# Softmax times values on one core: table load ahead of the wait, and the value copies of the next pass moved into the last head

## The chip, the cores and the metric

The kernel runs on one core of one Trainium2 chip. The metric is device time in microseconds (us), the median of several executions. "DVE" is VectorE, "ACT" ScalarE, "PE" TensorE, "POOL" GpSimd, and "SP" the engine that issues the DMAs. In the views "PEld" is the loading of weights into PE, and a "q" behind a name (SPq) stands for that engine's instruction queue.

## The reference

For 8 x 12 = 96 heads it takes a 1024 x 1024 score matrix and a 1024 x 64 value matrix, in float32:

```python
scores_max = np.max(scores, axis=-1, keepdims=True)
attn = np.exp(scores - scores_max)
attn = attn / (np.sum(attn, axis=-1, keepdims=True) + 1e-8)
return np.matmul(attn, v).astype(np.float32)
```

The kernel leaves the maximum out (the scores are normal random numbers) and gets the row sums from an extra column of ones beside the values.

## The kernel before

A loop of 24 passes handles four heads (k = 0 to 3) per pass, each head in eight rows of tiles (r = 0 to 7). Each row goes through ACT (exp), PE (eight transposes into PSUM, where its results land), DVE (copy to `pt`), PE (eight matmuls with the values) and, once or twice per head, DVE (reciprocal and product, `normalise`). Matmuls of a row are issued two rows late (`LAG = 2`). Each of the four heads has one 4 MB score buffer, which SP refills for the next pass once its exp is done.

The values are loaded for four heads at once (`load_v`), cast to float16 by POOL (`cast_v`), and "spread" by DVE: four copies per head put them into that head's `vones` buffer.

```python
    def spread_v(k, s, behind=None):
        copy = nc.vector.tensor_copy(
            out=vones_bufs[k][s * Q : (s + 1) * Q, :, 0:D].rearrange(
                "i (h l) d -> i h l d", l=L
            ),
            in_=v_half[k * Q : (k + 1) * Q, :, s],
        )
        if behind is not None:
            after(copy, behind)
...
    def heads(n0):
        for k in range(AHEAD):
            if k == 0:
                for s in range(S):
                    spread_v(k, s)              # four copies at the head of the pass
            st = dict(vones=vones_bufs[k])
            for r in range(R):
                ...                             # exp of two rows, eight transposes
                pt = take(pt_bufs)
                copy = nc.vector.tensor_copy(out=pt[:], in_=psT[:])
                if k < AHEAD - 1 and r % (R // S) == 0:
                    spread_v(k + 1, r // (R // S), copy)    # the next head's, in every second row
                ...
                pending.append((n0, k, r, pt, st))
                if len(pending) > LAG:
                    finish(pending.pop(0))      # matmuls, and normalise at the end of a head
        while pending:
            finish(pending.pop(0))
        cast_v()
        last(n0)                                # loads for the next pass, second store
```

`last` has a special case for the last pass but one: it cuts the final head's load into pieces of four, two, one and one rows, so that the end of the run need not wait for a whole tile.

The softmax here doesn't subtract the row's maximum and nothing guards it: scores larger than these inputs give would overflow.

Of the kernel before, what the change touches and what calls it, by code (L numbers as in the profile page):

```python
# [9 lines left out]
FP16 = mybir.dt.float16  # L10
EXP = mybir.ActivationFunctionType.Exp
# [3 lines left out]
def kernel(  # L15
# [6 lines left out]
    nc = tc.nc  # L22
    P = 128
# [6 lines left out]
    R = SQ // P  # L30
# [5 lines left out]
    AHEAD = 4  # L36
    Q = P // AHEAD
    S = P // Q
# [16 lines left out]
    sb_pool = ctx.enter_context(tc.tile_pool(name="sbpool", bufs=1))  # L55
# [4 lines left out]
    order16 = const_pool.tile([P, P], FP16, name="order16")  # L60

    nc.vector.tensor_copy(  # L62
        out=order16[:].rearrange("p (t j) -> p t j", t=T),
        in_=ident32[:].rearrange("p (j t) -> p t j", t=T),
# [11 lines left out]
    def buffers(pool, count, shape, dtype, name):  # L76
        return [pool.tile(shape, dtype, name=f"{name}{k}") for k in range(count)]

    s_bufs = buffers(sb_pool, AHEAD, [P, R, SK], FP32, "s_nat")
    v_sb = sb_pool.tile([P, C // L, S, L, D], FP32, name="v_sb")  # L80
    v_half = sb_pool.tile([P, C // L, S, L, D], FP16, name="v_half")
    p_bufs = buffers(sb_pool, 8, [P, EB, SK], FP16, "p_nat")
    pt_bufs = buffers(sb_pool, 4, [P, SK], FP16, "pt")
    out_bufs = buffers(sb_pool, 2, [P, T, R, D], FP32, "out_sb")
# [8 lines left out]
    def take(bufs):  # L93
        k = turn.get(id(bufs), 0)
        turn[id(bufs)] = k + 1
        return bufs[k % len(bufs)]
# [4 lines left out]
    def after(a, b):  # L101

        tc.add_manual_dep(
            a.ins,
            b.ins.name,
            mybir.DependencyInfo(mybir.DependencyClass.NoSync, mybir.DependencyReason.DATA),
            reason="order",
        )

    def queue(dma):  # L110

        if queued:
            after(dma, queued[-1])
        queued.append(dma)
# [4 lines left out]
    def normalise(k, st, first, last):  # L119

        psO = psO_whole if k % 2 == 0 else psO_banks[first]
        psO = psO[:, :, 0 : G * M].rearrange("p b (g m) -> p b g m", m=M)
        recip = st["recip"][:, first:last]
        nc.vector.reciprocal(out=recip, in_=psO[:, :, :, D : D + 1])  # L124
        h = k % T
        for t in range(T):
            part = slice(t * W, (t + 1) * W)
            rows = st["out_sb"][h * W : (h + 1) * W, t, first * G : last * G, :]
            nc.vector.tensor_tensor(  # L129
                out=rows.rearrange("j (b g) d -> j b g d", g=G),  # L130
                in0=psO[part, :, :, 0:D],
                in1=recip[part].to_broadcast([W, last - first, G, D]),
                op=mybir.AluOpType.mult,
            )

    def finish(u):

        n0, k, r, pt, st = u
        b, g = r // G, r % G
        if r == 0:  # L140
            st["recip"] = take(rc_bufs)
            st["out_sb"] = out_bufs[k // T]
        bank = psO_whole[:, b] if k % 2 == 0 else psO_banks[b][:, 0]
        for c in range(C):
            nc.tensor.matmul(  # L145
                out=bank[:, g * M : (g + 1) * M],
                lhsT=pt[:, c * P : (c + 1) * P],
                rhs=st["vones"][:, c, 0:M],
                start=(c == 0),
                stop=(c == C - 1),  # L150
            )
        if k % 2 == 1:
            if g == G - 1:
                normalise(k, st, b, b + 1)
        elif r == R - 1:
            normalise(k, st, 0, R // G)
        if r == R - 1 and k == T - 1:
            store(n0, 0)

    def store(n0, k):  # L160

        rows = out_bh.rearrange("(m x) y -> m x y", x=P)
        dma = nc.sync.dma_start(
            out=rows[bass.ds((n0 + k) // T, 1)].rearrange("o x y -> (o x) y"),
            in_=out_bufs[k // T][:].rearrange("x t r d -> x (t r d)"),
        )
        for other in stores:
            apart(dma, other)
            apart(other, dma)
        apart(dma, dma)  # L170
        stores.append(dma)
        queue(dma)
# [8 lines left out]
    def load(k, n, parts=(R,), r=0, **cond):  # L181
        for rows in parts:
            queue(
                nc.sync.dma_start(  # L184
                    out=s_bufs[k][:, r : r + rows, :],
                    in_=one(sc_bh, n)[:, r : r + rows, :],
                    **cond,
                )
            )
            r += rows  # L190

    def load_v(n):

        rows = v_bh.rearrange("(m x) y -> m x y", x=P)
        queue(
            nc.sync.dma_start(  # L196
                out=v_sb[:].rearrange("x h s l d -> x (h s l d)"),
                in_=rows[bass.ds(n // AHEAD, 1)].rearrange("o x y -> (o x) y"),
            )
        )  # L200

    def cast_v():
        nc.gpsimd.tensor_copy(out=v_half[:], in_=v_sb[:])  # L203
# [12 lines that stand above are left out]
    def load_next(k, n0):  # L216

        if k < AHEAD - 2:
            load(k, (n0 + (AHEAD + k)) % BH, cond=n0 < BH - AHEAD)

    def last(n0):


        before = queued[-1:]

        with tc.If(n0 < BH - 2 * AHEAD) as cmp:  # L226
            queued[:] = before
            load(AHEAD - 2, (n0 + (2 * AHEAD - 2)) % BH)
            load_v((n0 + 2 * AHEAD) % BH)
            load(AHEAD - 1, (n0 + (2 * AHEAD - 1)) % BH)  # L230
            store(n0, AHEAD - T)
        with cmp.Else():
            with tc.If(n0 < BH - AHEAD) as cmp2:
                queued[:] = before
                load(AHEAD - 2, BH - 2, (4, 4))
                load(AHEAD - 1, BH - 1, (4,))
                store(n0, AHEAD - T)
                load(AHEAD - 1, BH - 1, (2, 1, 1), 4)
            with cmp2.Else():
                queued[:] = before  # L240
                store(n0, AHEAD - T)

    def heads(n0):

        for k in range(AHEAD):
            if k == 0:
                for s in range(S):
                    spread_v(k, s)
            st = dict(vones=vones_bufs[k])
            for r in range(R):  # L250
                if r % EB == 0:
                    p_nat = take(p_bufs)
                    rows = 1 if k == AHEAD - 1 and r == R - EB else EB
                    for g in range(0, EB, rows):
                        nc.scalar.activation(  # L255
                            out=p_nat[:, g : g + rows, :].rearrange(
                                "p r (x v) -> p x r v", v=Q * L
                            ),
                            in_=s_bufs[k][:, r + g : r + g + rows, :].rearrange(
                                "p r (i x l) -> p x (r i) l", i=Q, l=L  # L260
                            ),
                            func=EXP,
                        )
                p_row = p_nat[:, r % EB, :].rearrange("p (h q l) -> p h l q", q=P, l=L)
                psT = take(psT_bufs)
                for c in range(C):
                    nc.tensor.transpose(  # L267
                        out=psT[:, c * P : (c + 1) * P],
                        in_=p_row[:, c // L, c % L, :],
                        identity=order16[:],  # L270
                    )
                pt = take(pt_bufs)
                copy = nc.vector.tensor_copy(out=pt[:], in_=psT[:])  # L273
                if k < AHEAD - 1 and r % (R // S) == 0:
                    spread_v(k + 1, r // (R // S), copy)
                if r == R - 1:
                    load_next(k, n0)
                pending.append((n0, k, r, pt, st))
                if len(pending) > LAG:
                    finish(pending.pop(0))  # L280
        while pending:
            finish(pending.pop(0))
        cast_v()
        last(n0)

    assert BH % AHEAD == 0 and BH >= 2 * AHEAD and SK == Q * S * C
    load_v(0)
    for k in range(AHEAD):
        load(k, k)
    cast_v()  # L290
    load_v(AHEAD)
    with tc.For_i(0, BH, AHEAD, iteration_sync="reg_based") as n0:  # L292
        queued.clear()
        heads(n0)
# [30 lines left out]
```

## Time and profile before

| | before |
|---|---|
| time, median of the first 3 executions | 1065.76 us (1065.69 to 1065.81) |
| span of the profile | 1064.0 us |
| a pass in the middle of the run | 43.69 us |
| DMA share and rate in that pass | 1.00, 432 GB/s |
| busiest compute engine | DVE, 74% |
| bytes of a pass | 18.87 million |

The DMA moves 18.87 MB per pass at 432 GB/s, and that takes the whole pass. The compute engines have 11 us of slack or more in each pass and matter only where the DMA has nothing left to do, at the end of the run.

### The profile page before, as it was taken

The numbers are of one execution on the slowest core, as the hardware profiler recorded it, in microseconds if no ns is written. First come the engines' busy times: TensorE is split into PE (matmuls) and PEld (weight loads), VectorE is DVE, ScalarE is ACT, GpSimd is POOL, SyncE is SP. The second block draws the span as 40 slices with busy tenths as digits, with TensorE's granted clock in tenths as the row PEclk, the third lists the DMA queues.
The fourth block names the chain that finished last, engine by engine and source line by source line (L and its number), as shares of the span: only waits on it lengthen the run. The fifth ranks groups of instructions, "written<-read, shape, count | busy, mean of one in ns | idle before, by whom it ended". The sixth has DMA issues, their size and how long they took to land.

```text
span 1064.0 us, 32161 instructions
## 1 busy us (share of the span) xinstructions
PE 731.4 (69%) x12288; PEld 678.4 (64%) x12288; DVE 786.6 (74%) x1589; ACT 735.6 (69%) x432; POOL 48.1 (5%) x31
## 2 busy tenths in 40 slices
PE   2766766767766677677686776867666777666676
PEld 2665756667666667666575665767565666666675
DVE  3776876868768777677786776868768687687777
ACT  3766776666767668586676866667766668676685
POOL 0000000000000000000000000000000000000000
PEclk9888888878889888888988888888889788898989
DMA  9999999999999999999999999999999999999995
GB/s 397 431 418 434 426 433 434 433 434 432 432 434 432 425 443 430 429 431 428 433 431 436 432 434 434 431 434 424 441 427 434 432 426 435 432 432 428 440 425 236
DMA packets 24772, 453.06 MB, mean 426 GB/s; under 512 B 2752, under 2 KB 2752, under 8 KB 9152
## 3 DMA queue, kind: packets, MB, share of 16 engines
q1 hardware_dynamic: 24768, 453.00, 99.2%
q8 instruction: 4, 0.07, 0.0%
HBM read 436.21 MB, written 25.17 MB: 434 GB/s over the span
## 4 chain that ended last, share of the span: by engine, by line
DMA 81%; ACT 12%; issue 3%; ACTq 1%; PE 1%; DVE 0%; SPq 0%; PEld 0%; DVEq 0%
DMA s_nat<-in_scores_dram 81%; ACT p_nat L255 12%; PE psT L267 1%; ACTq L255 1%; ACTq L226 0%; ACTq L292 0%; PE psO L145 0%; DVE pt L273 0%; PE psO_whole L145 0%; SPq L184 0%; PEld L267 0%; ACTq L320 0%; DVE out_sb L129 0%; SPq L196 0%; PEld L145 0%
## 5 line engine op out<-in xcount | busy, mean ns | idle before, releaser
L255 ACT ACTIVATE p_nat<-s_nat 128x2048 f16<-128x2048 f32 (+1 forms) x408 | 704.8, 1799 | 228.1 <-DMA s_nat<-in_scores_dram 202.2
L267 PE MATMUL psT<-order,p_nat 128*128 128x128 f16 x6144 | 574.9, 246 | 269.9 <-ACT p_nat L255 263.9
L273 DVE COPY pt<-psT 128x1024 f16<-128x1024 f16 x768 | 515.8, 687 | 200.6 <-PE L267 109.4
L267 PEld LDWEIGHTS <-p_nat 128*128 128x128 f16 x6144 | 446.5, 123 | 298.3 <-ACT p_nat L255 295.7
L145 PEld LDWEIGHTS <-pt 128*128 128x128 f16 x6144 | 302.9, 107 | 81.0 <-DVE pt L273 77.7
L145 PE MATMUL psO<-vones,pt 128*128 128x65 f16 x3072 | 177.4, 201 | 53.9 <-DVE pt L273 50.2
L145 PE MATMUL psO_whole<-vones,pt 128*128 128x65 f16 x3072 | 189.9, 211 | 2.7 <-DVE pt L273 2.4
L207 DVE COPY vones<-v_half 32x512 f16<-32x512 f16 x384 | 109.4, 285 | 22.8 <-POOL v_half L203 6.0
L255 ACT ACT_TABLE_LOAD x24 | 30.8, 1283 | 89.8 <-DMA s_nat<-in_scores_dram 81.7
L203 POOL CAST v_half<-v_sb 128x2048 f16<-128x2048 f32 x25 | 47.4, 1896 | 1002.3 <-DVE vones L207 957.1
L129 DVE TENSOR_TENSOR out_sb<-psO,recip 64x256 f32<-64x256 f32 x192 | 81.1, 423 | 6.1
L129 DVE TENSOR_TENSOR out_sb<-psO_whole,recip 64x512 f32<-64x512 f32 x96 | 66.1, 688 | 3.0
L124 DVE RECIPROCAL recip<-psO 128x4 f32<-128x4 f32 x96 | 17.1, 178 | 34.4 <-PE psO L145 17.6
L124 DVE RECIPROCAL recip<-psO_whole 128x8 f32<-128x8 f32 x48 | 9.7, 203 | 4.5 <-PE psT L267 3.9
L71 DVE MEMSET vones<- 128x16 f16 x4 | 0.2, 72 | 0.8 <-PEq L309 0.8
L62 DVE CAST order<-ident 128x128 f16<-128x128 f32 x1 | 0.2, 227 | 0.4 <-POOL ident masks.py:199 0.4
masks.py:199 POOL TENSOR_SCALAR_AFFINE_SELECT ident<-ident 128x128 f32<-128x128 f32 x1 | 0.3, 295 | 0.1
masks.py:197 POOL MEMSET ident<- 128x128 f32 x1 | 0.2, 205 | 0.3 <-POOLq L309 0.3
L309 POOL MEMSET const-float32-0.0<- 128x1 f32 x1 | 0.1, 100 | 0.2 <-issue 0.2
L309 POOL MEMSET const-bfloat16-1.0<- 128x1 bf16 x1 | 0.1, 103 | 0.0
L309 POOL MEMSET const-uint8-127<- 128x1 uint8 x1 | 0.1, 103 | 0.0
L309 POOL MEMSET const-float32-1.0<- 128x1 f32 x1 | 0.1, 100 | 0.0
## 6 DMA issues: line engine op xcount, KB each, us to landing
s_nat<-in_scores_dram SPq DMA_DIRECT2D x96, 4096.0 KB, 35.8
v_sb<-in_v_dram SPq DMA_DIRECT2D x24, 1024.0 KB, 33.1
out_dram<-out_sb SPq DMA_DIRECT2D x48, 512.0 KB, 26.9
s_nat<-in_scores_dram SPq DMA_DIRECT2D x3, 2048.0 KB, 32.4
s_nat<-in_scores_dram SPq DMA_DIRECT2D x1, 1024.0 KB, 25.4
s_nat<-in_scores_dram SPq DMA_DIRECT2D x2, 512.0 KB
```

The costliest lines, as they stand in the source:

```text
L62: nc.vector.tensor_copy(out=order16[:].rearrange("p (t j) -> p t j", t=T), in_=ident32[:].rearrange("p (j t) -> p t j", t=T),)
L71: nc.vector.memset(vo[:, :, D : D + 2], 1.0)
L124: nc.vector.reciprocal(out=recip, in_=psO[:, :, :, D : D + 1])
L129: nc.vector.tensor_tensor(out=rows.rearrange("j (b g) d -> j b g d", g=G), in0=psO[part, :, :, 0:D], in1=recip[part].to_broadcast([W, last ...
L145: nc.tensor.matmul(out=bank[:, g * M : (g + 1) * M], lhsT=pt[:, c * P : (c + 1) * P], rhs=st["vones"][:, c, 0:M], start=(c == 0), stop=(c ...
L203: nc.gpsimd.tensor_copy(out=v_half[:], in_=v_sb[:])
L207: copy = nc.vector.tensor_copy(out=vones_bufs[k][s * Q : (s + 1) * Q, :, 0:D].rearrange("i (h l) d -> i h l d", l=L), in_=v_half[k * Q : ( ...
L255: nc.scalar.activation(out=p_nat[:, g : g + rows, :].rearrange("p r (x v) -> p x r v", v=Q * L), in_=s_bufs[k][:, r + g : r + g + rows, :] ...
L267: nc.tensor.transpose(out=psT[:, c * P : (c + 1) * P], in_=p_row[:, c // L, c % L, :], identity=order16[:],)
L273: copy = nc.vector.tensor_copy(out=pt[:], in_=psT[:])
L309: nc = _bacc.Bacc("TRN2", target_bir_lowering=False, num_devices=1)
```

## The change

It has two aims. First, the exp table is loaded once per pass. The load stands ahead of the first exp, behind that exp's wait for data. A one-column exp that needs no data is put in front and takes the table load into the wait. Second, four spread copies at the head of each pass delay the first row's work on DVE. They are made earlier: the values of heads 0 and 1 of the next pass are spread during head 3 of this one. For that, heads 2 and 3 get theirs in heads 0 and 1, and the cast moves to the end of head 1.

```diff
+    spare = sb_pool.tile([P, 1], FP16, name="spare")
...
     def heads(n0):
+        table = nc.scalar.activation(out=spare[:], in_=order16[:, 0:1], func=EXP)
         for k in range(AHEAD):
-            if k == 0:
-                for s in range(S):
-                    spread_v(k, s)
...
-                        nc.scalar.activation(
+                        exp = nc.scalar.activation(
...
+                        if k == r == g == 0:
+                            after(exp, table)
...
-                if k < AHEAD - 1 and r % (R // S) == 0:
-                    spread_v(k + 1, r // (R // S), copy)
+                if k < 2 and r % 2 == 0:
+                    spread_v(k + 2, r // 2, copy)
+                elif k == AHEAD - 1:
+                    spread_v(r // S, r % S, copy)
...
+            if k == 1:
+                cast_v()
         while pending:
             finish(pending.pop(0))
-        cast_v()
         last(n0)
...
     cast_v()
+    for k in range(2):
+        for part in range(S):
+            spread_v(k, part)
     load_v(AHEAD)
```

More of the change, by code (lines that the diff above doesn't have):

```diff
@@ L280, in heads @@
                     finish(pending.pop(0))
+            if k == 1:
+                cast_v()
         while pending:
             finish(pending.pop(0))
-        cast_v()
         last(n0)
+    assert AHEAD == S == 4 and R == 2 * S
     assert BH % AHEAD == 0 and BH >= 2 * AHEAD and SK == Q * S * C
```

## The prediction

> **What bounds the kernel now.** I read the page first: busy shares, then the row of DMA shares in forty slices. No compute engine is above 74%. The DMA row is at nine tenths in every slice but the last, and one queue takes nearly all of the sixteen engines' time.
>
> ```profile
> PE 731.4 (69%) x12288; PEld 678.4 (64%) x12288; DVE 786.6 (74%) x1589; ACT 735.6 (69%) x432; POOL 48.1 (5%) x31
> ...
> DMA  9999999999999999999999999999999999999995
> ...
> q1 hardware_dynamic: 24768, 453.00, 99.2%
> ```
>
> An average can hide a pause at each pass of the loop, and the change is aimed at exactly such a place. So the second view was the busy time by stretch. Columns: stretch, its length, busy time (and count) of PE, PEld, DVE, ACT, POOL; then PE clock, DMA share, GB/s. The first two rows are whole passes, the others the end of the run.
>
> ```profile
> 500.00:543.69 43.69, 30.75 (x518) 28.53 (x516) 32.71 (x66) 30.60 (x19) 1.90 (x1) 0.85 1.00 432
> ...
> 923.70:967.40 43.70, 30.51 (x512) 28.45 (x512) 32.73 (x66) 30.62 (x19) 1.90 (x1) 0.85 1.00 432
> ...
> 1046.00:1050.00 4.00, 3.01 (x61) 2.70 (x62) 3.88 (x8) 3.94 (x3) 0.92 (x1) 1.00 0.83 344
> 1050.00:1055.00 5.00, 4.42 (x95) 4.07 (x92) 4.84 (x9) 3.55 (x3) 0.98 (x1) 1.00 0.33 137
> 1055.00:1059.00 4.00, 1.37 (x26) 0.92 (x24) 3.12 (x9) 0.00 (x0) 0.00 (x0) 1.00 0.00 0
> ```
>
> A pass takes 43.69 us with DMA share 1.00. Its bytes: four score tiles of 4096 KB, 1024 KB of values, two stores of 512 KB (the list of DMA issues), together 18 MB = 18.87 million bytes. At 432 GB/s that is 43.69 us: the whole pass. There is no room in it for a wait of the memory traffic.
>
> The third view was the chain of waits, because it looks as if it contradicted this (start us, length us, what):
>
> ```profile
> 880.31 5.60 ACT p_nat L255 x4
> 886.04 36.03 DMA s_nat<-in_scores_dram
> 922.64 0.14 issue
> ...
> 923.99 5.60 ACT p_nat L255 x4
> ```
>
> Read alone, it says that exp must finish before the next load can be issued, and that a shorter exp stage would shorten the period of 923.99 - 880.31 = 43.68 us. But the 36 us are not the time of one load: 4.19 MB at 432 GB/s take 9.7 us, so a load spends some 26 us behind other loads in the queue. If exp frees the buffer sooner, the load is issued sooner and stands in the queue longer by as much.
>
> What is not bound by DMA is the end. The last data have arrived by 1052, yet the last vector instruction ends at 1059.2. The timeline of DVE there has almost no gap (start, length, what):
>
> ```profile
> 1048.55 0.29 DVE L207 COPY vones<-v_half 32x512 f16<-32x512 f16 x1
> 1048.87 1.90 DVE L273 COPY pt<-psT 128x1024 f16<-128x1024 f16 x3
> 1050.80 0.21 DVE L124 RECIPROCAL recip<-psO_whole 128x8 f32<-128x8 f32 x1
> 1051.03 0.69 DVE L273 COPY pt<-psT 128x1024 f16<-128x1024 f16 x1
> 1051.76 1.41 DVE L129 TENSOR_TENSOR out_sb<-psO_whole,recip 64x512 f32<-64x512 f32 x2
> ...
> 1056.69 0.69 DVE L273 COPY pt<-psT 128x1024 f16<-128x1024 f16 x1
> 1058.10 0.18 DVE L124 RECIPROCAL recip<-psO 128x4 f32<-128x4 f32 x1 [0.72 <-PE psO L145]
> ```
>
> The last exp ends at 1053.55 and the last copy of transposed weights starts only at 1056.69: **VectorE bounds the tail**, with its one real gap the 0.72 us wait for the last eight matmuls.
>
> **What the Trainium skill says.** "DMA: Bandwidth & Descriptors", section "Where 436 GB/s comes from", gives a ceiling of 435.2 GB/s for a core's sixteen engines; the trace's 432 in whole passes is 99% of it, so it agrees that nothing is left there. "HBM Reference", section "Specifications (TRN2)", says that a core streaming alone measures about 425 GB/s, bounded by its DMA engines; the page's mean over the span, head and tail included, is 426. "ScalarE: Activation LUTs", section "What ACT_TABLE_LOAD costs", has about 1283 ns for the load plus a drain of about 1380 ns. The trace has 1283 ns for each of 24 loads; the drain is not seen here: one load starts at 540.06 for 1.28 us and the exp behind it at 541.35. "Perfetto Trace Analysis", section "Identifying the Most-Contended Engine", says to improve the most contended engine first; here that is the DMA, and the change takes nothing from it.
>
> **The change, part by part.**
> 1. **Table load.** Now the loop has its table load ahead of the first exp, behind that exp's wait for data: 81.7 us of waiting over 23 passes, then 1.28 us of loading with data in hand. With the one-column exp ahead of it, which needs only a constant, the load falls into that wait (3.56 us at 540.06). So it leaves ACT's path in 23 passes: 23 x 1.28 = 29.4 us. The small exp is not in the old trace; the shortest part of an exp group seen is 1.04 us for 1024 columns, so one column is an estimate of at most some tenths of a us, within the same wait. Worth to the end time: nothing, because exp only releases a buffer whose next load waits in a full queue.
> 2. **Spreading at the head of a pass.** Now four copies at 1.23 us in all stand ahead of the pass's first copy of transposed weights (500.17 to 501.40). They go: 24 x 1.23 = 29.5 us of DVE leave that place, and eight copies (about 2.3 us) are added once before the loop, while the first scores are still on their way (first exp at 15.3 us). Worth to the end: nothing, for the same reason.
> 3. **Where they reappear.** Spread copies per pass were 4 at the head and 4 each in heads 0, 1, 2. Then they are 4 each in heads 0 and 1, none in head 2 and 8 in head 3, one per row. The number per pass stays 16 at 285 ns.
> 4. **Cast.** It moves from the end of a pass to the end of head 1. Now POOL waits 957 us of the span for the last spread, and the queue's view shows 97.3 us, 4.2 per pass, in which the load of values stands waiting for this cast. That wait goes, but the queue behind is full: no gain.
> 5. **The tail.** Only this is on the path that sets the end. In the last pass the eight copies of head 3 serve a pass that never comes, but they run. From the timeline one spread copy moves what follows by about 0.32 us: 1045.27 to 1046.91 is 1.64 us for a spread and two copies, and two copies take 1.29, the rest 0.03 being dead time. Head 2 loses four: 4 x 0.32 = 1.26 us earlier. Not all of it counts: exp for the first rows of head 3 ends only at 1047.88 and eight transposes follow (about 0.5 us), so their copy cannot start before some 1048.5; it starts now at about 1049.5, since the line at 1048.87 holds head 2's last row first. Gain about 1.0. Head 3 gets seven copies ahead of its last row: 7 x 0.32 = 2.2 us later. The eighth lies beside the last matmuls, in the 0.72 us gap. Net: 2.2 - 1.0 = **+1.2 us**.
>
> Sum: 1065.76 + 1.2 = 1067.0 us.
>
> **Rivals.**
> A. *The chain is real and the queue is not full.* Then table load and head spread would come off 23 passes, up to 23 x (1.28 + 1.23) = 58 us, near 1008 us. For it: the chain of waits passes through exp in every pass, and PE waits 295.7 us for exp. Against it: DMA share 1.00 at 432 GB/s, and bytes over rate give the pass to within 0.01 us. I give it 1%.
> B. *VectorE becomes the bound in head 3, and holds up the store and the loads behind it.* In the pass at 531 head 3 is already the crowded one: exp is over at 536.5, the last normalising ends at 543.7. Eight copies make that up to 2.5 us later, and the second store with it. But loads already issued keep the queue busy for 25 us and more (the shortest time to landing at the end is 25.4 us), so a store that is late by 2.5 us leaves no hole. VectorE's sum per pass stays 32.7 of 43.69 us. Only if the delay grew from pass to pass would it cost; the waits for data at heads 1 and 3 clear it. If it did cost some, 1069 to 1072.
> C. *The tail gets nothing.* If the compiler puts the copies elsewhere, or PE and not DVE sets the last rows, the time stays at 1065.8. Against it: PE has waits for DVE in these rows, and the copies are pinned behind the row's copy.
> D. *The clock of TensorE.* It is at 1.00 throughout the old tail, but drops to 0.50 for some us in other passes (500 to 502, 530 to 537). The new rhythm could move such a drop into the tail: with PE rows about twice as long, 1 to 2 us more.
>
> **Range and chances.** Three runs before lie within 0.12 us, so the range is that of my sum: from C (1065.6) to the whole of +2.2 with a touch of D (1068.4). The 2% borders are at 1044.4 and 1087.1, and only A or a grave form of B gets there: faster 0.01, same 0.98, slower 0.01.
>
> **What would show it.** DMA share and GB/s of whole passes stay at 1.00 and 432, period 43.69 us. The table loads' idle time is no longer a wait for score data, and the first exp of a pass starts about 1.3 us sooner after its data, while a load's time from issue to landing grows by about as much for that buffer. DVE's tail has a 0.29 us copy behind each copy of head 3, and the last normalising starts 1.2 us later against the last landing. The cast no longer makes the value load wait. I am wrong if whole passes become shorter than 43.6 us (A), if DMA share falls below 0.99 in them (B), or if the tail after the last landing is not longer (C).

## The result, and the profile after

The changed kernel takes 1068.09 us (1067.65 to 1068.40, four runs) against 1065.72 us (1065.51 to 1065.81, four runs): 2.37 us more. The ratio is 1.0022, with a 95% interval of 1.0005 to 1.0040. A ratio is the mean time of one kernel's runs over that of the other's in the same rounds, so it is not quite the ratio of the medians. By the 2% rule this is the same time, but the small loss is clear of noise.

The page of the changed kernel, in the same rows as before, shows a DMA that is as busy as it was:

```profile
PE 740.1 (69%) x12288; PEld 687.1 (64%) x12288; DVE 792.6 (74%) x1597; ACT 740.9 (70%) x456; POOL 48.1 (5%) x31
...
DMA  9999999999999999999999999999999999999995
...
q1 hardware_dynamic: 24768, 453.00, 99.1%
```

The busy time by stretch of the changed kernel (columns as in the prediction) has the same whole passes. Only the end differs. Between 1055 and 1059 DVE is busy for 3.78 us, where it was 3.12, and its last instruction ends at 1061.06, where it ended at 1059.19:

```profile
500.00:543.69 43.69, 30.62 (x512) 28.37 (x512) 33.06 (x67) 30.88 (x20) 1.90 (x1) 0.85 1.00 432
...
923.70:967.40 43.70, 30.61 (x512) 28.25 (x512) 33.00 (x66) 30.77 (x20) 1.90 (x1) 0.85 1.00 432
...
1055.00:1059.00 4.00, 1.44 (x27) 0.92 (x24) 3.78 (x10) 0.00 (x0) 0.00 (x0) 0.98 0.01 2
1059.00:1064.00 5.00, 0.62 (x8) 0.46 (x8) 1.54 (x5) 0.00 (x0) 0.00 (x0) 0.50 0.25 105
```

The first aim was reached. The groups of ACT instructions, first of the kernel before, then of the changed one, give busy time and mean length, then the idle time just before the group and what ended it:

```profile
L255 ACT ACTIVATE p_nat<-s_nat 128x2048 f16<-128x2048 f32 (+1 forms) x408 | 704.8, 1799 | 228.1 <-DMA s_nat<-in_scores_dram 202.2 <-SPq L226 25.6
L255 ACT ACT_TABLE_LOAD x24 | 30.8, 1283 | 89.8 <-DMA s_nat<-in_scores_dram 81.7 <-SPq L292 8.1
```

```profile
L255 ACT ACTIVATE p_nat<-s_nat 128x2048 f16<-128x2048 f32 (+1 forms) x408 | 705.1, 1800 | 311.0 <-DMA s_nat<-in_scores_dram 257.0 <-SPq L227 53.6 <-PE L269 0.4
L247 ACT ACT_TABLE_LOAD x24 | 30.8, 1283 | 1.8 <-ACTq L303 1.4
L247 ACT ACTIVATE spare<-order 128x1 f16<-128x1 f16 x24 | 4.9, 206 | 0.3
```

The table load no longer waits: its 89.8 us of idle time became 1.8. But the exp behind it waits 311.0 us where it waited 228.1. A wait changed its owner. ACT idled for 317.9 us in these rows, and now for 313.1.

The other aim, a DVE free at the head of a pass, was paid for at the end of the run. DVE's timeline in the changed kernel's tail (start, length, what) has the new copies (L208) in it:

```profile
1051.10 0.21 DVE L125 RECIPROCAL recip<-psO_whole 128x8 f32<-128x8 f32 x1
1051.23 0.64 DVE L275 COPY pt<-psT 128x1024 f16<-128x1024 f16 x1
1051.78 1.40 DVE L130 TENSOR_TENSOR out_sb<-psO_whole,recip 64x512 f32<-64x512 f32 x2
1053.21 0.28 DVE L208 COPY vones<-v_half 32x512 f16<-32x512 f16 x1
1053.53 0.69 DVE L275 COPY pt<-psT 128x1024 f16<-128x1024 f16 x1
1054.25 0.29 DVE L208 COPY vones<-v_half 32x512 f16<-32x512 f16 x1
...
1058.53 0.69 DVE L275 COPY pt<-psT 128x1024 f16<-128x1024 f16 x1
1059.25 0.29 DVE L208 COPY vones<-v_half 32x512 f16<-32x512 f16 x1
1059.97 0.18 DVE L125 RECIPROCAL recip<-psO 128x4 f32<-128x4 f32 x1 [0.43 <-PE psO L146]
```

From the reciprocal of head 2 to the start of the last row's copy it is now 1058.53 - 1051.10 = 7.43 us. Before it was 1056.69 - 1050.80 = 5.89 us. Five spread copies lie in between, and 1.54 / 5 = 0.31 us for each. This stretch is a good ruler for the tail, and I measured it in the experiments with full bytes. It depends little on when the last data land or on how far behind DVE was when it got there: without copies in it, it is 5.71 to 6.00 us in the runs below. A second measure takes these in: from the first exp of head 3 (1045.96 before, 1046.22 changed) to the end of the last vector instruction (1059.19 and 1061.06), which is 13.23 us before and 14.84 changed.

### The profile page after: what moved, and what is told of

It reads as the page before. It is cut to its first block, busy times and chain, and to the rows that moved or that the text cites. A ratio compares the mean times of both kernels' runs of the same rounds, so it can differ in the third digit from the quotient of the medians.

```text
span 1065.6 us, 32145 instructions
## 1 busy us (share of the span) xinstructions
PE 740.1 (69%) x12288; PEld 687.1 (64%) x12288; DVE 792.6 (74%) x1597; ACT 740.9 (70%) x456; POOL 48.1 (5%) x31
## 4 chain that ended last, share of the span: by engine, by line
DMA 79%; ACT 13%; issue 3%; PE 2%; ACTq 1%; DVE 1%; PEld 1%; SPq 0%; DVEq 0%
DMA s_nat<-in_scores_dram 79%; ACT p_nat L255 13%; PE psT L269 1%; DVE pt L275 1%; ACTq L255 1%; PE psO_whole L146 1%; PE psO L146 0%; PEld L269 0%; ACTq L227 0%; SPq L185 0%; ACTq L303 0%; PEld L146 0%; DVE out_sb L130 0%; ACTq L331 0%; DVE vones L208 0%
## 5 line engine op out<-in xcount | busy, mean ns | idle before, releaser
L255 ACT ACTIVATE p_nat<-s_nat 128x2048 f16<-128x2048 f32 (+1 forms) x408 | 705.1, 1800 | 311.0 <-DMA s_nat<-in_scores_dram 257.0
L269 PE MATMUL psT<-order,p_nat 128*128 128x128 f16 x6144 | 567.5, 248 | 229.1 <-ACT p_nat L255 225.5
L275 DVE COPY pt<-psT 128x1024 f16<-128x1024 f16 x768 | 523.4, 688 | 213.3 <-PE L146 86.2
L269 PEld LDWEIGHTS <-p_nat 128*128 128x128 f16 x6144 | 452.8, 124 | 251.1 <-ACT p_nat L255 245.4
L146 PE MATMUL psO<-vones,pt 128*128 128x65 f16 x3072 | 183.8, 205 | 89.1 <-DVE pt L275 87.7
L146 PE MATMUL psO_whole<-vones,pt 128*128 128x65 f16 x3072 | 184.1, 208 | 1.6 <-DVE pt L275 1.0
L208 DVE COPY vones<-v_half 32x512 f16<-32x512 f16 x392 | 111.6, 285 | 18.6 <-POOL v_half L204 7.2
L247 ACT ACT_TABLE_LOAD x24 | 30.8, 1283 | 1.8 <-ACTq L303 1.4
L247 ACT ACTIVATE spare<-order 128x1 f16<-128x1 f16 x24 | 4.9, 206 | 0.3
## 6 DMA issues: line engine op xcount, KB each, us to landing
s_nat<-in_scores_dram SPq DMA_DIRECT2D x96, 4096.0 KB, 35.8
```

The source lines that it names most:

```text
L146: nc.tensor.matmul(out=bank[:, g * M : (g + 1) * M], lhsT=pt[:, c * P : (c + 1) * P], rhs=st["vones"][:, c, 0:M], start=(c == 0), stop=(c ...
L208: copy = nc.vector.tensor_copy(out=vones_bufs[k][s * Q : (s + 1) * Q, :, 0:D].rearrange("i (h l) d -> i h l d", l=L), in_=v_half[k * Q : ( ...
L247: table = nc.scalar.activation(out=spare[:], in_=order16[:, 0:1], func=EXP)
L255: exp = nc.scalar.activation(out=p_nat[:, g : g + rows, :].rearrange("p r (x v) -> p x r v", v=Q * L), in_=s_bufs[k][:, r + g : r + g + ro ...
L269: nc.tensor.transpose(out=psT[:, c * P : (c + 1) * P], in_=p_row[:, c // L, c % L, :], identity=order16[:],)
```

## The experiments

The theory: the DMA queue is full, so nothing that shortens ACT's or DVE's path within a pass counts, and the loss comes from the spread copies in head 3 of the last pass. Its rivals are those of the prediction: exp is on the path of every pass (A), the copies cost in every pass (B), or the loss has nothing to do with these copies but with the table exp or the new rhythm.

All timed runs had three or five rounds beside the kernel before. Its median was 1065.72 to 1065.79.

**1. The one-column exp alone** (kernel before, plus `spare`, `table` and the order behind it; the spread copies stay where they were).

> The kernel before with the one-column exp alone. Theory (full DMA queue; only the tail of the last pass counts): table loads move into the wait for data, whole passes stay 43.69 us at 432 GB/s, time within 0.4 us of before (1065.7). Rival A (exp is on the path of every pass): 23 x 1.28 = 29 us less, near 1036.

Measured: 1065.77 us, ratio 0.9999 (0.9986 to 1.0013). The stretch in the tail is 5.90 us. Taking 1.28 us off ACT in every pass is worth nothing.

**2. The spread copies and the cast alone.**

```diff
-        table = nc.scalar.activation(out=spare[:], in_=order16[:, 0:1], func=EXP)
...
-                        if k == r == g == 0:
-                            after(exp, table)
```

> The changed kernel without the one-column exp: only the move of the spread copies and of the cast. Theory: the whole loss is here, 1068.1 +- 0.4, as the changed kernel, with its last vector instruction about 1.9 us later than before in the profile. If the small exp or the table load took part in the loss, the time lies clearly between 1065.7 and 1068.1.

Measured: 1067.84 us, ratio 1.0019 (1.0006 to 1.0033), with the stretch at 7.43 us as in the changed kernel. The last vector instruction ends 2.2 us later than before, and 0.5 us of that is a later start of head 3 (1046.44). So the loss is in the move of the copies and of the cast, and no part of the table exp in it is seen. No run moved the cast alone. Run 3 below adds copies with the cast left where it is.

**3. The copies of head 3 made twice.**

```diff
                 elif k == AHEAD - 1:
                     spread_v(r // S, r % S, copy)
+                    spread_v(r // S, r % S, copy)
```

> The changed kernel with every spread copy of head 3 done twice, 8 more copies of 285 ns in each of 24 passes. Theory (they cost only in the last pass's tail, seven of them at 0.32 us): 1068.1 + 2.2 = 1070.3. If the copies cost in every pass (rival B), 24 x up to 2.5 us, some 1090 to 1128. If the loss is not from these copies at all: 1068.1.

Measured: 1071.37 us, 3.3 us above the changed kernel where 2.2 were expected. The stretch is 9.33 us. More copies in head 3 make the end later, and DVE's work per pass is 2 us more (34.98 against 33.06 us from 500 to 543.69) at the same 43.69 us per pass, so whole passes pay nothing. The surplus of about 1 us goes with a backlog. In the last pass but one, head 3 ends later too: its store is issued at 1026.97, and at 1025.01 in the changed kernel. The last pass starts with that debt, and the first copy of its head 3 starts 4.9 us after its exp, where it was 2.9. In this profile head 3's exp itself starts 0.5 us earlier (1045.70), which hides part of these 2 us.

**4. Exp made longer at the head of each pass** (on two new buffers of 2048 columns).

```diff
+        for _ in range(2):
+            extra = nc.scalar.activation(out=busy_out[:], in_=busy_in[:], func=EXP)
+            after(extra, table)
+            table = extra
```

> The changed kernel with two useless exps of 2048 columns (1.9 us each) at the head of every pass, behind the one-column exp. About 2 us of the 3.8 fall into ACT's wait for data, the other 1.8 delay head 0's exp and so the issue of the next load. Theory (the queue is full): the load is issued later and waits less, whole passes stay 43.69 us, time 1068.1 +- 0.5. Rival A: 23 x 1.8 = 41 us more, near 1109.

Measured: 1068.39 us, against 1068.09 for the changed kernel. 24 x 3.8 = 91 us of useless exps were added, and 0.3 us came of it, with the two ranges overlapping. In the trace one of the two went ahead of head 0's first exp and one behind it; head 0's last three exps start at 980.39 where they started at about 978.6. So some 1.8 us of the 3.8, 43 us in the run, delay head 0's exp, and the rest falls into its wait. Whole passes stay at 43.69 us. This speaks directly against rival A: the chain of waits passes through exp in every pass, and a longer exp does not make the pass longer.

**5. No value loads in the loop** (wrong result).

```diff
-            load_v((n0 + 2 * AHEAD) % BH)
```

> The changed kernel without the 22 loads of values in the loop (wrong result on purpose; the casts read old values). Theory (bytes over rate): 22 x 1.0486 MB at 432 GB/s = 53.4 us less, 1068.1 - 53.4 = 1014.7, passes of 41.26 us. Rival A (latency of a chain through exp): little or no change, above 1055.

Measured: 1018.19 us, 49.9 less than the changed kernel. This row of its busy time by stretch has the shorter pass with the DMA as full as before:

```profile
500.00:541.26 41.26, 30.05 (x512) 27.67 (x512) 32.66 (x68) 30.76 (x19) 1.89 (x1) 0.83 1.00 432
```

The first exp of the last head starts at 991.84, 54.4 us earlier, where bytes over rate gave 53.4. The tail behind it takes 19.8 us in place of 14.8 and gives 5.0 of these back. Bytes set the passes, and the compute tail comes on top.

**6 and 7. Half of the score bytes: before and changed** (only rows 0 to 3 of each tile are loaded in the loop, all arithmetic stays; wrong result). This asks whether the change would pay if the DMA were not the bound.

```diff
-    def load(k, n, parts=(R,), r=0, **cond):
+    def load(k, n, parts=(R,), r=0, half=True, **cond):
+        if half:
+            parts, r = ((R // 2,), 0) if r == 0 else ((), 0)
```

> The kernel before with only the first half of every score tile loaded in the loop (wrong result on purpose; all arithmetic stays). Bytes per pass 10.5 MB, 24.3 us at 432 GB/s, so compute sets the pass. Theory: a pass is then above 32.7 us (VectorE's busy time) and below 43.69, the run some 800 to 950 us, DMA share well below 1. This is the case in which the change should pay; compare with e7.

> The changed kernel with the same halved loads. Theory: with DMA no longer the bound, table load and head spread are on the path at each pass: up to 23 x 2.5 = 58 us less than e6, at least 15 us. If the change gains nothing even then, its intent was wrong for a reason other than the DMA, such as VectorE's sum, which it leaves alone (32.7 us per pass in both).

Measured: 859.40 us and 893.32 us. My expectation for the second was plainly wrong. I forecast at least 15 us of gain, and the change *loses* 34 us. The stretches show whole passes of each, first of the kernel before and then of the changed one:

```profile
388.10:422.45 34.35, 26.29 (x512) 23.22 (x512) 31.85 (x67) 31.05 (x18) 1.89 (x1) 1.00 0.77 305
```

```profile
400.50:436.05 35.55, 28.26 (x518) 24.95 (x515) 32.27 (x67) 30.96 (x21) 1.89 (x1) 0.90 0.74 295
```

DMA share is 0.77 and 0.74, so it is no longer the bound, and a pass is 1.2 us longer with the change. Other passes of the changed one are longer still: from one table load to the next, eighteen passes from the fourth on average 34.4 us before and 35.9 changed. Over 23 passes, 1.5 us each make the whole loss of 34. DVE's own rows say how, in the same order (idle time before the group, and what ended it):

```profile
L275 DVE COPY pt<-psT 128x1024 f16<-128x1024 f16 x768 | 503.9, 683 | 36.0 <-PE L145 13.0 <-PE L269 12.3 <-PE psO_whole L145 0.8
```

```profile
L277 DVE COPY pt<-psT 128x1024 f16<-128x1024 f16 x768 | 514.5, 685 | 68.9 <-PE L146 36.4 <-PE L271 17.4 <-PE psO_whole L146 4.6
```

DVE stands idle for 33 us more in front of the row copies, waiting for PE, and its copies themselves take 11 us more. (In front of its other work it idles some 11 us less.) Around the end of head 2, now without spread copies, its timeline has waits of 0.27 us for PE in front of single rows (at 407.75 and 408.71); in head 3 it has more work per row than before. The old placement, one copy in every second row, seems to have used such waits; that is a reading of the timelines and not tested. The granted PE clock is also lower (0.90 against 1.00). I did not separate the two.

**8. The last pass written out after the loop, without the useless copies** (the branches and the condition that chose the last loads go with it; not shown).

```diff
-                elif k == AHEAD - 1:
+                elif k == AHEAD - 1 and not final:
                     spread_v(r // S, r % S, copy)
...
-            if k == 1:
+            if k == 1 and not final:
                 cast_v()
...
-    with tc.For_i(0, BH, AHEAD, iteration_sync="reg_based") as n0:
+    with tc.For_i(0, BH - AHEAD, AHEAD, iteration_sync="reg_based") as n0:
         ...
+    heads(BH - AHEAD, final=True)
```

> The changed kernel with its last pass written out after the loop, without the eight spread copies and the cast that serve no pass. Theory: tail 7 x 0.32 = 2.2 us shorter, 1068.1 - 2.2 = 1065.9, perhaps a few tenths less than before, as head 2 has no spread copies either. If the loss comes from the rhythm of the passes and not from these copies: 1068.1 stays. Leaving the loop may cost a us of its own, hidden while loads are under way.

Measured: 1093.56 us, 28 us slower than before. As a test of the total this failed. ACT's timeline shows why:

```profile
1052.90 1.28 ACT L243 ACT_TABLE_LOAD   x1 [35.84 <-PEq L332]
```

ACT stood idle for 35.84 us between the loop and the written-out pass, and PE and DVE for 32. SP's queue waited at the line of the loop (L302) for score loads to land, 21.2 us in two waits. The last pass began only at 1052.9, with the DMA done (its share is 0.05 from 1050 to 1060). I had thought that leaving the loop "may cost a us of its own". One thing can still be read: without spread copies, the stretch in head 3 is 5.71 us (1080.29 to 1086.00).

**9 and 10. All copies early** (twelve in head 0, four in head 1, the cast after head 0; before the loop only head 0's four), to free both the head of the pass and the tail; and the same with the last head's first load in two pieces, `(2, 2)` for `(4,)`.

```diff
-                if k < 2 and r % 2 == 0:
-                    spread_v(k + 2, r // 2, copy)
-                elif k == AHEAD - 1:
-                    spread_v(r // S, r % S, copy)
+                if k == 0:
+                    if r < S:
+                        spread_v(1, r, copy)
+                    spread_v(2 + r // S, r % S, copy)
+                elif k == 1 and 3 <= r < 3 + S:
+                    spread_v(0, r - 3, copy)
...
-            if k == 1:
+            if k == 0:
                 cast_v()
```

> One-column exp kept; all spread copies early in the pass: 12 in head 0, 4 in head 1, none in heads 2 and 3 and none at the head of the loop; the cast after head 0. Theory: from the first exp of head 3 to the last normalising before 13.2 us, changed 14.8; without copies in head 3, and with VectorE ahead, 13.2 - 0.6 = 12.6 us, so 1065.1 +- 0.4. If the loss came from the loop's new rhythm or the cast's place and not from the copies in head 3: 1068. If copies in head 0 cost at each pass: above 1070.

> As e9, and the last head's first 2 MB load cut into two of 1 MB, so that exp of its first rows need not wait 1.1 us for four rows. Theory: with VectorE ahead, the tail starts up to 1.1 us sooner, 1064.0 to 1065. If VectorE still is the bound there: as e9.

Measured: 1074.33 and 1073.87 us. Both missed, by my own making. The values for the next pass land only in the middle of a pass, some 32 us after their issue. I asked for them in head 1, and DVE waited for the cast there, with row copies behind:

```profile
DVE vones L208 <- POOL v_half L204: 195.2, 24, 17.2
```

In 24 waits DVE stood still for 195 us in all (17.2 the longest, at the start; 5.64 in the last pass). The chain of waits now runs through the value load and the cast in most passes. The loss of 8.6 us shows in two places. After two passes at the start, ten still take 43.7 us from table load to table load, but the last eleven take 43.96, some 3 us in all. And the tail from the first exp of head 3 (1049.15) to the last vector instruction (1067.82) takes 18.7 us, where it took 13.2. The changed kernel asks for these values in head 3, and its only such waits are two with 7.2 us in all, 6.0 of them before the loop. The stretch in head 3, which has no copies here, is again 6.00 us. Cutting the load (run 10) brought 0.5 us, with overlapping ranges, in a kernel that had other trouble; what it is worth elsewhere stays open.

**11 and 12. Half of the bytes again, with the one-column exp alone and with the copies early** (wrong results).

> The kernel before with the one-column exp alone and halved score loads (wrong result on purpose). With e6 (859.4, before) and e7 (893.3, changed): if the copies in head 3 cause the 34 us, this stays at 859 or gains up to some us; if the early table load (exp running further ahead) causes them, it is near 893.

> The kernel of e9 with halved score loads (wrong result on purpose). Theory (copies between the last rows of a head-3 hold up the last matmuls, and with them the next pass): at or below 859, up to 30 us less. If any move of the copies away from the head of the loop loses: near 893.

Measured: 858.61 and 887.90 us. The one-column exp is worth at most 0.8 us even where compute is the bound (859.40 without it; DVE is the busiest engine and ACT has waits for PE to fall into). So the 34 us of run 7 belong to the moved copies and cast, which this pair does not separate, alone or together with the exp. Moved early instead of late they also lose, 28 us, against my expectation. There, too, DVE idles more: 46.5 us in front of row copies and 35.0 in front of spread copies, 23.1 of these waiting for the cast, where the kernel before has 36.0 and 22.9. But 16.9 of the 23.1 are one wait at the start of the run. The passes themselves average 35.2 us, against 34.4.

**The ruler over all runs with full bytes.** Spread copies in head 3 of the last pass against the stretch from the reciprocal of head 2 to the last row's copy:

| run | copies per row of head 3 | stretch, us | time, us |
|---|---|---|---|
| before | 0 | 5.89 | 1065.72 |
| 1, one-column exp alone | 0 | 5.90 | 1065.77 |
| 8, last pass apart | 0 | 5.71 | 1093.56 |
| 9, copies early | 0 | 6.00 | 1074.33 |
| 10, early, small loads | 0 | 6.00 | 1073.87 |
| changed | 1 | 7.43 | 1068.09 |
| 2, spread move alone | 1 | 7.43 | 1067.84 |
| 4, exp longer | 1 | 7.43 | 1068.39 |
| 3, copies twice | 2 | 9.33 | 1071.37 |

The ruler goes with the number of copies and not with the place of the cast, which is moved in all of these runs but the first two. It does not go with the total: runs 8, 9 and 10 lost elsewhere, so no run took the copies out of the tail and got the time back.

With full bytes no run beat the kernel before. A version that asks for head 0's values in head 2, after their landing and ahead of the tail, is the next thing to try; it was not run.

## Why the prediction was right, and where it was off

The time, 1067.0 with a range of 1065.6 to 1068.4, holds the measured 1068.09. The direction and the mechanism were right; the size of the loss was 2.4 us where 1.2 was said.

That the range held is partly luck. Its upper part stood for a tail without any gain and a touch of a lower clock; what came was a tail with a smaller gain, and 0.8 us that the sum did not have (below).

*The bound* held: whole passes are 43.69 us at 432 GB/s and share 1.00 in both. Runs 4 and 5 tested it from both sides: more exp costs nothing, fewer bytes save what they should in the passes.

*Part 1, the table load,* was right: off ACT's path, worth nothing (run 1). The first exp of a pass starts 1.29 us sooner (976.77, and 978.06 before), and the small exp measures 0.21 us. One sign named for it did not appear: score loads still take a median of 35.8 us from issue to landing, and the next load of head 0 is issued at 987.77, where it was 987.84. In the changed kernel 24 issues of score loads wait for the landing of another score load (81.9 us), where it was 3 (24.7 us). Run 2 has these waits too (81.8 us) and run 1 does not (24.5), so they come with the moved copies and not with the small exp; yet the load is issued no sooner in run 1 either (987.76). So for the scores the reason given, issued sooner and longer in the queue, is not what the trace shows. What holds the loads there I did not find out.

*Parts 2 and 3* were right for the passes: four copies left their head, 16 per pass remained, and the period is the same.

*Part 4, the cast,* was right, and here the sign did appear. The load of values, no longer waiting 4.2 us for the cast, takes 4.2 us longer to land:

```profile
v_sb<-in_v_dram SPq DMA_DIRECT2D x24, 1024.0 KB, 33.1
```

```profile
v_sb<-in_v_dram SPq DMA_DIRECT2D x24, 1024.0 KB, 37.3
```

These are the issues of the kernel before and of the changed one, with the median time to landing last. Issued sooner, landed at the same place in the queue.

*Part 5, the tail,* was right in its cost and wrong in its gain. "[S]even copies ahead of its last row: 7 x 0.32 = 2.2 us later" is what the trace has. The first row's copy of head 3 starts at 1049.10 and the last row's ends at 1059.22, 10.1 us. Before, these were 1049.48 (the second of three copies in the line at 1048.87) and 1057.38, 7.9 us. (The prediction's 4 x 0.32 is 1.28 and not 1.26, which changes nothing.) The term that failed is "Gain about 1.0" for head 2. The first row's copy starts 0.38 us sooner, or 0.64 counted from the first exp of head 3. I had allowed 0.6 us from the end of the first exp to that copy; in the trace it is 0.96 (1048.14 to 1049.10). Two of DVE's waits for PE, of 0.27 us each, took the place of copies removed from head 2. So the tail behind the first exp grew by 2.22 - 0.64 = 1.6 us, which is what 14.84 - 13.23 gives.

The rest, 2.37 - 1.6 = 0.8 us, is settled in part. The two profiled runs differ by 1067.65 - 1065.76 = 1.89 us, and their last vector instructions by 1.87: the 1.6 of the tail and 0.26 by which head 3's first exp starts later. The other 0.5 us lies within the scatter of the runs: the profiled run of the changed kernel is the fastest of its four. The later start comes for the most part from the last two whole passes, which take 43.78 and 43.79 us from table load to table load, where those before them average 43.67. In run 2 the last five are about 43.8, in runs 3 and 4, with as many copies or more, none is. So the start is not shown to belong to the copies, and its cause is open.

Rival D was near but cost next to nothing: the PE clock falls to 0.50 from 1059 on, and the last eight matmuls take 0.62 us, where they took 0.43 at 1.00 (1.4 times as long, where the prediction said about twice). But the eighth spread copy lies beside them, and the time from the end of the last row's copy to the reciprocal is 0.75 us against 0.72.

Rival A is out (runs 1, 4 and 5). Rival B is out in the form that was feared, a cost in every pass (run 3); the 0.26 us above is all that could be left of it. Rival C is out (run 2, and the ruler).

## What to carry to other kernels

Before moving work off the head of a loop, look at whether the stretch around it has a DMA share of 1.00: here a shorter wait only changed its owner in such a stretch, though the chain of waits named exp in every pass. Then look at the last pass, where the DMA is done and the new place of the work has no cover: work done "for the next pass" is pure cost there. And where compute is the bound, moving copies can cost in every pass: 34 us late and 28 us early in the half-byte runs. That they had filled regular short waits before is a likely reason, not a tested one.

## What the Trainium skill lacked or had wrong

- **"ScalarE: Activation LUTs", section "What ACT_TABLE_LOAD costs":** for a switch to a different set of functions it gives a load of about 1283 ns plus a drain of about 1380 ns. It does not say what a repeated load costs when no other function is used, as in this kernel, which uses exp alone. The load is 1283 ns in all 24 cases, and no drain is seen beside it: in one pass the exp before ends at 973.28, the load starts at 973.30, and the small exp starts at 974.59, 1.29 us later.
- **No page that I read has the cost of leaving a loop while loads are under way.** In run 8 the engines stood still until the DMA was done, 35.84 us for ACT and 32 us for PE and DVE.
- **"Perfetto Trace Analysis", section "Identifying Dependency Chains":** it tells how to find what an instruction waits for, but not how to tell a chain that sets the time from one that only follows a full queue. Here 91 us of added exps, some 43 of them on that chain, cost 0.3 us (run 4), and the value load that was issued 4.2 us sooner took 4.2 us longer to land.
